# A two-layer diffusion backbone: the end of the first layer's expert mixture, with gates per expert and the overflow loop ahead of the last two experts

## The chip, the cores and the metric

The kernel runs on one core of one Trainium2 chip. The metric is device time in microseconds; the time before is the median of three runs. Engines are called as in the profile: PE (TensorE, matmuls), PEld (its weight loads), DVE (VectorE), ACT (ScalarE), POOL (GpSimd) and SP (SyncE, which here issues most DMA transfers).

## The reference, cut to what matters

Two layers, each a token mixer and then a mixture of experts, over 256 context and 256 latent tokens of width 1024. In the first layer both sets of tokens go through the mixture (512 tokens); each token goes to two of 32 experts. Context and latent tokens have gates of their own (`cgate2`, `gate2`).

```
def layer step (layer 0, second half):
    h = concat([layer_norm(xc) * (1 + cscale2) + cshift2, layer_norm(x) * (1 + scale2) + shift2])
    ffn = moe(h)          # sum over a token's two experts of w * (silu(h Wg) * (h Wu)) Wd
    xc = post_norm(ALPHA * xc + cgate2 * ffn[:256], ln2_g, ln2_b)
    x  = post_norm(ALPHA * x  + gate2  * ffn[256:], ln2_g, ln2_b)
```

Then layer 1 begins with `layer_norm` of both, a modulation, and the product with `w_in`.

## The kernel before

`moe(rt, keep)` is written once for both layers; `l` is the layer, and the change concerns `l == 0`, with `nt` = 4 tiles of 128 tokens. Tokens are gathered by expert in blocks of 64 rows. The loop runs over 34 experts: 0 to 19, then 32 and 33 (two spare blocks for experts with more than 64 tokens), then 20 to 31. An expert's weights are six loads of 1 MB (two halves each of gate, up and down), issued by SP in `load` (L1681) into a ring of 11 buffers. A load is issued when its buffer is free and when the transfer eight places earlier on SP has landed, since SP's transfers take turns on eight semaphores.

The work of one expert `e` in `expert0`: POOL gathers its tokens (L1688, `xg`), PE transposes them (`pxt`), ACT copies them out (`xgt`), PE forms gate and up in one PSUM tile (`pgu`, L1731), ACT and DVE make the SwiGLU (`th`, L1696 and L84), PE transposes it (`pat`, L1740), and PE multiplies by the down weights (`pd`, L1751). PE's order is interleaved: while expert `e` waits for its SwiGLU, gate of `e + 1` runs. ACT scales the result by the routing weight (`ye`, L93), and POOL scatters it to `yb_d` in DRAM (L1791), one row per token and choice.

Experts 30 and 31 don't go through DRAM. Their result stays as two rounded parts, `yh` (ACT) and `yl` (DVE), and PE multiplies both by a one-hot matrix `slt` into `po` (L1940), one 128x512 result for each tile and half; DVE adds these to `fa`, the sum of the token tile.

Behind that: `overflow` (L1514 on), a hardware loop over blocks that found no place in the spare ones. Its trip count is read from `ovi`, and with these inputs it is zero. Then the tail for each tile: gate (`g`), residual (`fx`, from `x1_d`, times `ALPHA`), statistics (L225, L226), affine step with `lg` and `lb`, and the store `x_d`. Layer 1's mixer normalises these tiles again (`bnnb`, `xh` on ACT, L242), transposes them on PE (`pht`, L482), and multiplies by `w_in` (`raw`, L516, split into `hi` on ACT and `lo` on DVE; `pfm`, L526 to L528).

Order around the change: a scheduler sets the order on each engine when the kernel is built. It doesn't move anything across a hardware loop. At the loop all engines meet, on the skip path too: SP goes on when the transfers that it issued have landed, and the others when everybody has arrived.

Of the kernel before, what the change touches and what calls it, by code (L numbers as in the profile page):

```python
# [11 lines left out]
F32 = mybir.dt.float32  # L12
# [9 lines left out]
D = 1024  # L22
# [30 lines left out]
def trunk(ctx: ExitStack, tc: tile.TileContext, A, out):  # L53
# [1285 lines left out]
    def route_start(l):  # L1339
        nt = 4 - 2 * l  # L1340

        def new(shape, name, dt=F32):
            return const.tile(shape, dt, tag="rt_" + name, name=name)

        rt = dict(l=l, nt=nt, both=new([128, 4, 32], "both")[:, :nt], ovi=new([1, 24], "ovi", I32))
        if l == 0:
            rt.update(oh=[new([128, 4, 32], f"oh{k}") for k in range(2)], wgt=new([128, 3, 4], "wgt"),
                      pos=new([128, 2, 4], "pos"), idx=new([128, 2, 32], "idx", I32), tok=new([128, 2], "tok"), wsl=new([128, 32], "wsl"),
                      sidx=new([128, 2, 2], "sidx", I32), swsl=new([128, 2], "swsl"),
                      pidx=pb("pidx")[:, :96])  # L1350
        else:

            rt.update(posx=new([128, 4, 32], "oh0")[:, :nt], wx=new([128, 4, 32], "oh1")[:, :nt])
        return rt
# [84 lines left out]
    def route_end(rt, wk):  # L1439
        if rt["l"] == 0:  # L1440
# [7 lines left out]
            V.tensor_copy(rt["wsl"], rt["pidx"][:, 64:96])  # L1448
            V.tensor_copy(rt["tok"], val[:, 0, 30:32])

    def route_over(rt, wk):
# [33 lines left out]
        for b in range(ns):  # L1485
# [23 lines left out]
            ts(val[:, 1:2], val[:, 1:2], 2.0, second, OP.mult, OP.add)  # L1509
            V.tensor_copy(rt["sidx"][:, :, b], val)  # L1510
            V.tensor_copy(rt["swsl"][:, b:b + 1], pi[:, 2:3])

    def overflow(rt, acc, g2):
# [4 lines left out]
        with ExitStack() as ph:  # L1518
            wk = ph.enter_context(tc.tile_pool(name=f"ov{l}", bufs=1))
            n = nc.values_load(ovi[0:1, NB:NB + 1], min_val=0, max_val=NB - ns)  # L1520
            with tc.For_i(0, n, 1) as b:  # L1521
# [75 lines left out]

                pg, pu = pa("pog"), pa("pou")
                for p, w in ((pg, A["moe_w_gate"]), (pu, A["moe_w_up"])):
# [11 lines left out]
                for nh in range(2):  # L1611
                    raw = load(A["moe_w_down"][l, ds(eb, 1), :, 512 * nh:512 * nh + 512])
                    p = pa("pod")
                    for k in range(4):
                        T.matmul(p[:rows], at_[:, k], raw[:, k], start=(k == 0), stop=(k == 3))
                    copyS(y[:rows, 512 * nh:512 * nh + 512], p[:rows], scale=wcol[:rows])
                slt = wk.tile([128, nt, 128], F32, name="oslt")
                if l == 0:
# [8 lines left out]
                for t in range(nt):  # L1627
                    for nh in range(2):
                        po = pc("opo")
                        cs = slice(512 * nh, 512 * nh + 512)  # L1630
                        T.matmul(po, slt[:rows, t], y[:rows, cs], start=True, stop=True)
                        if l == 1:
                            yg = wk.tile([128, 512], F32, tag="oyg", name="oyg")
                            tt(yg, po, g2[1][:, cs], OP.mult)
                            po = yg
                        tt(acc[t][:, cs], acc[t][:, cs], po, OP.add)

    def moe(rt, keep):
# [26 lines left out]
        if l == 0:  # L1665
            xg = [fx.tile([128, D], F32, name=f"xg{i}") for i in range(2)]
            for i in range(2):
                G.memset(xg[i], 0.0)
        else:
            acc = [fx.tile([128, D], F32, name=f"acc{t}") for t in range(nt)]  # L1670
# [100 lines left out]
        def expert0(e, xt, pgu, nxt):  # L1771
            y = wk.tile([128, 512], F32, tag="y", name="ye", bufs=3) if e not in (30, 31) else None
            front = nxt()
# [8 lines left out]
            down(p, e, a)  # L1782
            w = rt["wsl"][:, e:e + 1] if e < 32 else rt["swsl"][:, e - 32:e - 31]
            if e in (30, 31):
                yh, yl = y2[e - 30]
                copyS(yh, p, scale=w)
                stt(yl, p, w, yh, OP.mult, OP.subtract)
                return front
            copyS(y, p, scale=w)
            i = rt["idx"][:, 1, e:e + 1] if e < 32 else rt["sidx"][:, 1, e - 32:e - 31]  # L1790
# [110 lines left out]
        if l == 0:  # L1901

            pr3.close()
            bc = keep.enter_context(tc.tile_pool(name=f"fbc{l}", bufs=1, side="right", reuse_waits="tile"))
            pl2 = ExitStack()
            lp_ = pl2.enter_context(tc.tile_pool(name="last", bufs=1, side="right", reuse_waits="tile"))
            acc = [bc.tile([128, D], F32, name=f"fa{t}") for t in range(nt)]
            y2 = [[lp_.tile([128, 512], F32R, name=f"y{n}{i}") for n in "hl"] for i in range(2)]
# [8 lines left out]
        with tc.issue_after(rt["load"].ins):  # L1917
            if l == 0:
                xs = [bc.tile([128, D], F32, name=f"fx{t}") for t in range(2)]
                for t in range(2):  # L1920
                    y1 = lp_.tile([128, D], F32, tag="y1", name="y1", bufs=2)
                    for i, y in enumerate((acc[t], y1)):
                        dma(y, yb_d[ntok * i + 128 * t:ntok * i + 128 * t + 128, :])
                    tt(acc[t], acc[t], y1, OP.add)
                for t in range(2):
                    dma(xs[t], x1_d[128 * t:128 * t + 128, :])
                for t in range(2, nt):
                    dma(acc[t], yb_d[128 * t:128 * t + 128, :])
                g2 = {0: mod_bc(bc, l, 5, 0, "g20")}
            lg = bc_row(bc, part_bcast(A["ln2_g"][l], 128), "lg2")  # L1930
            lb = bc_row(bc, part_bcast(A["ln2_b"][l], 128), "lb2")
# [14 lines left out]
        pwk.close()  # L1946
        overflow(rt, acc, g2)
        fp = keep.enter_context(tc.tile_pool(name=f"fin{l}", bufs=2, side="right", reuse_waits="tile"))
        if l == 0:
            g2[1] = mod_bc(fp, l, 5, 1, "g21")  # L1950

        for t in range(nt):
            rows = slice(128 * t, 128 * t + 128)
            x = acc[t]
            if l == 0:
                f = tg if t else tt
                if t < 2:
# [98 lines left out]
```

## Time and profile before

| | us |
|---|---|
| runs: lowest, median, highest | 2517.08, 2523.96, 2527.08 |
| profiled execution, its own time | 2517.75 |
| its span | 2516.0 |
| PE busy | 2196.1 (87%) |
| DVE busy | 1414.9 (56%) |
| ACT busy | 693.1 (28%) |
| POOL busy | 544.6 (22%) |

The first mixture takes about 880 to 1434 us of the span, the seam behind it ends near 1487, where layer 1's first `pht` starts. The shares of the whole span mix stages with different limits, so the seam is read from rows of its own. The trace has two records for each of these matmul instructions: a half load of gate or up, eight instructions in the program, stands as x16.

### The profile page before, as it was taken

What the parts mean: (1) busy time and instruction counts of PE and PEld (TensorE: products, weight loads), DVE (VectorE), ACT (ScalarE), POOL (GpSimd) and SP (SyncE); (2) the same over time, 40 slices, a digit from 0 to 9 for tenths busy, and PEclk for the clock granted to TensorE, in tenths of its full rate; (3) what the DMA queues carried; (4) which work ended last, traced back from release to release, by engine and by line L of the source; (5) the groups of instructions that cost most, each with busy time, mean ns of one, the idle gap of its engine ahead of it and who ended that gap; (6) DMA issues with size and microseconds to landing.
All of it is one profiled execution on the core that took longest, in us unless ns stands there. A gap on an engine that the chain in (4) does not pass through costs nothing. (4 is left out here: it accounts for less than half of the span.)

```text
span 2516.0 us, 41430 instructions
## 1 busy us (share of the span) xinstructions
PE 2196.1 (87%) x16198; PEld 1525.2 (61%) x16198; DVE 1414.9 (56%) x2987; ACT 693.1 (28%) x1344; POOL 544.6 (22%) x486
## 2 busy tenths in 40 slices
PE   5899998999999699777688839997799779999996
PEld 3678766886657555444344437896777655555553
DVE  7958635657756720443432286456888755545445
ACT  2334412345552011111111113352365311111110
POOL 8989600022110301311011031001142100000000
PEclk8999999999999799889898969998899889999998
DMA  6643588657666699999999957649565699999996
GB/s 254 188 132 113 164 235 272 197 167 217 187 204 219 239 363 413 408 410 400 403 402 406 416 172 237 194 145 262 176 213 141 229 367 381 421 423 421 422 421 265
DMA packets 326999, 710.71 MB, mean 282 GB/s; under 512 B 40654, under 2 KB 240766, under 8 KB 274064
## 3 DMA queue, kind: packets, MB, share of 16 engines
q1 hardware_dynamic: 306576, 682.69, 75.4%
q10 hardware_dynamic: 14944, 17.27, 1.9%
q0 software_dynamic: 5280, 8.05, 1.0%
q8 instruction: 130, 2.13, 0.3%
q14 instruction: 69, 0.57, 0.1%
HBM read 645.82 MB, written 71.37 MB: 285 GB/s over the span
## 5 line engine op out<-in xcount | busy, mean ns | idle before, releaser
L1731 PE MATMUL pgu<-mraw,xgt 128*64 128x256 f32 x4224 | 507.3, 393 | 10.0 <-DMA mraw<-in_moe_w_up_dram 7.4
L1731 PEld LDWEIGHTS pgu<-mraw,xgt 128*64 128x64 f32 x4224 | 305.3, 141 | 193.1 <-issue 41.9
L526 PE MATMUL pfm<-hhi,hi 128*128 128x256 f32 (+1 forms) x832 | 284.0, 345 | 6.4 <-ACT hi L93 6.4
L528 PE MATMUL pfm<-hhi,lo 128*128 128x256 f32 (+1 forms) x832 | 281.8, 342 | 5.4 <-DVE lo L78 5.4
L527 PE MATMUL pfm<-hlo,hi 128*128 128x256 f32 (+1 forms) x832 | 284.1, 343 | 0.0
L78 DVE TENSOR_TENSOR lo<-raw,hi 128x1024 fp32r<-128x1024 f32 (+1 forms) x147 | 197.3, 1344 | 140.9 <-ACT hi L93 128.4
L1751 PE MATMUL pd<-mraw,at 128*64 128x512 f32 x1056 | 248.3, 604 | 17.4 <-ACT at L93 15.4
L93 ACT ACTIVATE hi<-raw 128x1024 fp32r<-128x1024 f32 (+1 forms) x160 | 169.3, 1059 | 222.0 <-PE pfm L527 119.6
L84 DVE SCALAR_TENSOR_TENSOR th<-th,pgu 128x256 f32<-128x256 f32 x132 | 55.5, 420 | 310.0 <-ACT th L1696 308.0
L526 PEld LDWEIGHTS pfm<-hhi,hi 128*128 128x128 f32 x832 | 158.6, 192 | 31.3 <-ACT hi L93 7.5
L528 PEld LDWEIGHTS pfm<-hhi,lo 128*128 128x128 f32 x832 | 158.4, 191 | 28.4 <-DVE lo L78 6.4
L527 PEld LDWEIGHTS pfm<-hlo,hi 128*128 128x128 f32 x832 | 158.9, 191 | 20.7 <-issue 4.7
L128 POOL TENSOR_TENSOR bnrs<-bnrs,mhalf 128x1 f32<-128x1 f32 x26 | 27.8, 1074 | 624.7 <-DVE bnrs L88 624.7
L1751 PEld LDWEIGHTS pd<-mraw,at 128*64 128x64 f32 x1056 | 72.4, 138 | 148.9 <-issue 108.2
L78 DVE TENSOR_TENSOR acc<-acc,po 128x512 f32<-128x512 f32 x124 | 79.6, 682 | 99.2 <-PE po L1839 99.1
L526 PE MATMUL pm<-yh,hi 128*128 128x512 f32 (+1 forms) x256 | 89.6, 363 | 8.8 <-DVE gatel L84 5.9
L527 PE MATMUL pm<-yl,hi 128*128 128x512 f32 (+1 forms) x256 | 90.8, 357 | 5.9 <-DVE yl L78 5.8
L526 PE MATMUL ptm<-hi,hhi 128*128 128x256 f32 x320 | 93.1, 291 | 0.0
L528 PE MATMUL ptm<-hi,hlo 128*128 128x256 f32 x320 | 92.7, 290 | 0.0
L84 DVE SCALAR_TENSOR_TENSOR yg<-pd,wcol,g 64x512 f32<-64x512 f32 x64 | 48.0, 750 | 78.8 <-PE pd L1751 78.4
L527 PE MATMUL ptm<-lo,hhi 128*128 128x256 f32 x320 | 92.2, 288 | 0.0
L528 PE MATMUL pm<-yh,lo 128*128 128x512 f32 (+1 forms) x256 | 88.8, 350 | 0.0
(533 smaller groups left out, 4131.0 us busy)
## 6 DMA issues: line engine op xcount, KB each, us to landing
mraw<-in_moe_w_gate_dram SPq DMA_DIRECT2D x132, 1024.0 KB
mraw<-in_moe_w_up_dram SPq DMA_DIRECT2D x132, 1024.0 KB
mraw<-in_moe_w_down_dram SPq DMA_DIRECT2D x132, 1024.0 KB
raw<-in_w_in_dram SPq DMA_DIRECT2D x116, 512.0 KB
modr<-in_mod_w_dram SPq DMA_DIRECT2D x80, 512.0 KB
modw<-in_mod_w_dram SPq DMA_DIRECT2D x8, 1024.0 KB
g_d<-gate SPq DMA_DIRECT2D x32, 256.0 KB
gtl<-gt_d SPq DMA_DIRECT2D x8, 1024.0 KB
```

The lines of the kernel that those rows point to most:

```text
L78: V.tensor_tensor(o, a, b, op=op)
L84: V.scalar_tensor_tensor(o, a, s, b, op0=op0, op1=op1)
L93: S.activation(o, a, AF.Copy, scale=scale)
L128: G.tensor_tensor(o, a, b, op=OP.pow)
L526: T.matmul(p, ahi, bhi, start=first, stop=False)
L527: T.matmul(p, ahi, blo, start=False, stop=False)
L528: T.matmul(p, alo, bhi, start=False, stop=last)
L1731: o = T.matmul(p[64 * cb:64 * cb + 64, 256 * i:256 * i + 256], xt[:, kt], raw[:, k, 256 * cb:256 * cb + 256], start=(kt == 0), stop=(kt == ...
L1751: o = T.matmul(p[64 * nh:64 * nh + 64], at[:, j, 64 * cb:64 * cb + 64], raws[cb][:, j, nh], start=(k == 0), stop=(k == 3))
```

## The change

1. `rt["cls"]` holds for each slot of each expert whether its token index is under 256 (context).
2. The gate is applied per expert: `g2n` holds both gate vectors in the layout of `pd`. For each expert DVE forms `gr` = gate vector by class (one tensor-scalar, one scalar-tensor-tensor and a 128x1 step) and `y` = `pd` times routing weight times `gr`. This takes the place of ACT's `ye` copy. For experts 30 and 31 `yh` is a copy of `y`, and `yl` the rest.
3. `fa` starts as `x1_d` times `ALPHA` (four loads by POOL's queue, four ACT steps), ahead of the loop.
4. `overflow` for layer 0 stands ahead of experts 30 and 31, and gates what it adds.
5. Behind expert 31, eight loads `ys` of `yb_d` by POOL's queue are added to `fa`: for tiles 0 to 2 by DVE, for tile 3 by POOL.
6. The tail's gates, residuals and `y` sums are gone, with their loads.

```
@@ route_end, route_over
+            ts(rt["cls"][:, :32], val[:, 0], 256.0, None, OP.is_lt)
+            ts(rt["cls"][:, 32 + b:33 + b], val[:, 0:1], 256.0, None, OP.is_lt)
@@ overflow
+                gg = g2
+                if l == 0:
+                    gg = [mod_bc(wk, l, 5, c, f"og{c}") for c in range(2)]
...
-                        if l == 1:
-                            yg = wk.tile([128, 512], F32, tag="oyg", name="oyg")
-                            tt(yg, po, g2[1][:, cs], OP.mult)
-                            po = yg
-                        tt(acc[t][:, cs], acc[t][:, cs], po, OP.add)
+                        yg = wk.tile([128, 512], F32, tag="oyg", name="oyg")
+                        tt(yg, po, gg[t // 2 if l == 0 else 1][:, cs], OP.mult)
+                        tt(acc[t][:, cs], acc[t][:, cs], yg, OP.add)
@@ moe
+            g2n = fx.tile([128, 2, 512], F32, name="g2n")
+            for c in range(2):
+                for nh in range(2):
+                    m = mods[0, 10 + nh, c, :]
+                    dma(g2n[64 * nh:64 * nh + 64, c], bass.AP(tensor=m.tensor, offset=m.offset, ap=[[0, 64], [1, 512]]))
@@ expert0
+            gr = wk.tile([128, 512], F32, tag="gr", name="gr", bufs=1)
+            c1 = wk.tile([128, 1], F32, tag="c1", name="c1")
+            ts(c1, rt["cls"][:, e:e + 1], -1.0, 1.0, OP.mult, OP.add)
+            ts(gr, g2n[:, 0], rt["cls"][:, e:e + 1])
+            stt(gr, g2n[:, 1], c1, gr, OP.mult, OP.add)
+            stt(y, p, w, gr, OP.mult, OP.mult)
             if e in (30, 31):
                 yh, yl = y2[e - 30]
-                copyS(yh, p, scale=w)
-                stt(yl, p, w, yh, OP.mult, OP.subtract)
+                copyS(yh, y)
+                tt(yl, y, yh, OP.subtract)
                 return front
-            copyS(y, p, scale=w)
@@ ahead of experts 30 and 31
+            acc = [bc.tile([128, D], F32, name=f"fa{t}") for t in range(nt)]
+            for t in range(nt):
+                G.dma_start(acc[t], x1_d[128 * t:128 * t + 128, :])
+                copyS(acc[t], acc[t], scale=ALPHA)
+            overflow(rt, acc, None)
@@ behind expert 31
-                xs = [bc.tile([128, D], F32, name=f"fx{t}") for t in range(2)]
-                for t in range(2):
-                    y1 = lp_.tile([128, D], F32, tag="y1", name="y1", bufs=2)
-                    for i, y in enumerate((acc[t], y1)):
-                        dma(y, yb_d[ntok * i + 128 * t:ntok * i + 128 * t + 128, :])
-                    tt(acc[t], acc[t], y1, OP.add)
...
+                for t in range(nt):
+                    for i in range(2):
+                        y = lp_.tile([128, D], F32, tag="ys", name="ys", bufs=6)
+                        G.dma_start(y, yb_d[ntok * i + 128 * t:ntok * i + 128 * t + 128, :])
+                        with tc.high_priority(offset=2000):
+                            (tg if t == 3 else tt)(acc[t], acc[t], y, OP.add)
...
-        overflow(rt, acc, g2)
+        if l:
+            overflow(rt, acc, g2)
...
-                f = tg if t else tt
-                if t < 2:
-                    f(x, x, g2[0], OP.mult)
-                    stt(x, xs[t], ALPHA, x, OP.mult, OP.add)
-                else:
-                    y = fp.tile([128, D], F32, tag="y", name="y")
-                    dma(y, yb_d[ntok + 128 * t:ntok + 128 * t + 128, :])
-                    f(x, x, y, OP.add)
-                    f(x, x, g2[1], OP.mult)
-                    xt = fp.tile([128, D], F32, tag="x", name="fx")
-                    dma(xt, x1_d[128 * t:128 * t + 128, :])
-                    stt(x, xt, ALPHA, x, OP.mult, OP.add)
             normed_affine(fp, x, x, lg, lb)
```

How the instructions stand now is shown at three places. A row is line, operation, result and operands, shape and count; `x8` of `pgu` is one half load. L1731, L1740, L1751 and L1940 of before are L1739, L1748, L1759 and L1954 of after.

PE before, from the transposes of expert 31's tokens on: first `pd` is expert 29's, the `x24` are both halves of `up` 30 and the first of gate 31, then `pd` of expert 30, its `po`, and `up` of 31. The loop stands some 30 rows further.

```order
L1760 MATMUL pxt<-identr,xg_8316 128x64 x8
L1731 MATMUL pgu<-mraw,xgt 64x256 x8
L1751 MATMUL pd<-mraw,at_11818 64x512 x8
L1731 MATMUL pgu<-mraw,xgt 64x256 x24
L1740 MATMUL pat<-identr,th 128x128 x2
L1731 MATMUL pgu<-mraw,xgt 64x256 x8
L1751 MATMUL pd<-mraw,at_11929 64x512 x8
L1940 MATMUL po<-yh_11851,slt 128x512
L1731 MATMUL pgu<-mraw,xgt 64x256 x8
L1940 MATMUL po<-yl_11852,slt 128x512
```

PE after, up to the loop: first the transpose of expert 29 and the last half of gate 30, `pd` of expert 29, and one half of `up` 30.

```order
L1748 MATMUL pat<-identr,th 128x128 x2
L1739 MATMUL pgu<-mraw,xgt 64x256 x8
L1759 MATMUL pd<-mraw,at_11982 64x512 x8
L1739 MATMUL pgu<-mraw,xgt 64x256 x8
L1522 TENSOR_LOAD ovi
L1523 COMPARE_AND_BRANCH
```

PE after, behind the loop: the transposes of expert 31's tokens, the other half of `up` 30 with the first of gate 31, then as before.

```order
L1768 MATMUL pxt<-identr,xg_8318 128x64 x8
L1739 MATMUL pgu<-mraw,xgt 64x256 x16
L1748 MATMUL pat<-identr,th 128x128 x2
L1739 MATMUL pgu<-mraw,xgt 64x256 x8
L1759 MATMUL pd<-mraw,at_12342 64x512 x8
L1739 MATMUL pgu<-mraw,xgt 64x256 x8
L1954 MATMUL po<-yh_12263,slt 128x512
L1954 MATMUL po<-yl_12264,slt 128x512
L1739 MATMUL pgu<-mraw,xgt 64x256 x8
```

So half of expert 30's work (half of `up`, and `down`) and all of expert 31's moved from ahead of the loop to behind it.

SP before, from expert 31's last four loads on (`up`, then `down`). The loop stands nine rows further.

```order
L1681 DMA mraw<-in_moe_w_up_dram 128x2048 x2
L1681 DMA mraw<-in_moe_w_down_dram 128x2048 x2
L1926 DMA fx_11992<-x1m_d 128x1024
L1926 DMA fx_11993<-x1m_d 128x1024
L213 DMA g_12006<-mods 128x2x512
L213 DMA lg_12008<-in_ln_g_dram 128x1024
L213 DMA lb_12010<-in_ln_b_dram 128x1024
L516 DMA raw<-in_w_in_dram 128x4x256 x3
L1923 DMA fa_11847<-yb_d 128x1024
```

SP after, from expert 31's gate on.

```order
L1689 DMA mraw<-in_moe_w_gate_dram 128x2048 x2
L1689 DMA mraw<-in_moe_w_down_dram 128x2048 x2
L1689 DMA mraw<-in_moe_w_up_dram 128x2048 x2
L1689 DMA mraw<-in_moe_w_down_dram 128x2048 x2
L213 DMA lg_12442<-in_ln_g_dram 128x1024
L213 DMA lb_12444<-in_ln_b_dram 128x1024
L1523 COMPARE_AND_BRANCH
L1523 UNCONDITIONAL_BRANCH x2
```

The weight loads keep their places, `fx` and `g` are gone, and the loop stands right behind `lb`; six `raw` follow behind the loop.

DVE before, from `yl` of expert 30 (`yl_11852`) to the loop; the four `fa` numbers are the four tiles.

```order
L84 SCALAR_TENSOR_TENSOR yl_11852<-pd,wsl,yh_11851 128x512
L84 SCALAR_TENSOR_TENSOR th<-th,pgu 128x256 x2
L84 SCALAR_TENSOR_TENSOR yl_11854<-pd,wsl,yh_11853 128x512
L78 TENSOR_TENSOR lo<-raw,hi 128x4x256 x3
L78 TENSOR_TENSOR fa_11847<-fa_11847,y_11994 128x1024
L78 TENSOR_TENSOR fa_11847<-fa_11847,po 128x512 x2
L78 TENSOR_TENSOR fa_11848<-fa_11848,y_11998 128x1024
L78 TENSOR_TENSOR fa_11848<-fa_11848,po 128x512 x2
L78 TENSOR_TENSOR fa_11849<-fa_11849,po 128x512 x2
L78 TENSOR_TENSOR fa_11850<-fa_11850,po 128x512 x2
L1520 TENSOR_LOAD ovi
```

DVE after, from `yl` of expert 31 (`yl_12266`) behind the loop to the first statistics; the four MEMSETs are short.

```order
L78 TENSOR_TENSOR lo<-raw,hi 128x4x256 x3
L78 TENSOR_TENSOR fa_12013<-fa_12013,ys 128x1024 x2
L78 TENSOR_TENSOR fa_12014<-fa_12014,ys 128x1024
L78 TENSOR_TENSOR fa_12013<-fa_12013,po 128x512 x2
L78 TENSOR_TENSOR fa_12014<-fa_12014,ys 128x1024
L78 TENSOR_TENSOR fa_12014<-fa_12014,po 128x512 x2
L78 TENSOR_TENSOR fa_12015<-fa_12015,ys 128x1024 x2
L78 TENSOR_TENSOR fa_12015<-fa_12015,po 128x512 x2
L78 TENSOR_TENSOR fa_12016<-fa_12016,po 128x512 x2
L225 BN_STATS bnst<-fa_12013 128x6
```

The sums, which stood ahead of the loop, stand behind it with six `ys` sums among them, and the statistics follow at once. POOL's order has the four `fa<-x1m_d` loads ahead of the scatters of experts 28 and 29, and these ahead of the loop; behind it come the eight `ys` loads and then the two sums of tile 3.

## Rows read from the trace of the kernel before

**Rows 1.** Windows in the mixture: stretch, length, busy us by engine, clock, DMA share, GB/s.
```profile
1180.00:1200.00 20.00, 16.52 (x128) 9.59 (x128) 1.78 (x4) 3.73 (x7) 2.93 (x3) 1.00 1.03 408
...
1380.00:1400.00 20.00, 20.00 (x152) 11.04 (x148) 0.84 (x2) 2.74 (x5) 2.02 (x2) 1.00 1.01 410
```

**Rows 2.** Waits in 900 to 1400: PE's, then SP's queue; total, times, longest.
```profile
PE pat L1740 <- DVE th L84: 40.7, 17, 8.7
...
SPq L1681 <- DMA mraw<-in_moe_w_gate_dram: 90.5, 28, 9.5
```

**Rows 3.** SP's issues at the seam: start, us, queue, line, operation, transfer, count.
```profile
1405.55 2.75 SPq L1681 DMA_DIRECT2D mraw<-in_moe_w_down_dram  x2
...
1418.33 0.33 SPq L213 DMA_DIRECT2D lg<-in_ln_g_dram  x1
1420.83 0.33 SPq L213 DMA_DIRECT2D lb<-in_ln_b_dram  x1
1423.50 7.94 SPq L516 DMA_DIRECT2D raw<-in_w_in_dram  x3
```

**Rows 4.** Timeline, experts 30 and 31: start, us, engine, instruction, idle before and releaser.
```profile
1413.91 0.51 PE L1740 MATMUL pat<-identr,th 128*128 128x128 f32 x2
...
1418.36 1.94 PE L1751 MATMUL pd<-mraw,at 128*64 128x512 f32 x8 [0.35 <-DMA mraw<-in_moe_w_down_dram]
...
1421.52 1.95 PE L1731 MATMUL pgu<-mraw,xgt 128*64 128x256 f32 x16
...
1433.48 0.75 DVE L84 SCALAR_TENSOR_TENSOR yl<-pd,wsl,yh 128x512 fp32r<-128x512 f32 x1 [6.38 <-ACT yh L93]
```

**Rows 5.** Windows at the seam: PE, PEld, DVE, ACT, POOL busy, clock, DMA.
```profile
1449.00:1455.00 6.00, 0.00 (x0) 0.00 (x0) 0.72 (x3) 0.00 (x0) 0.14 (x1) 0.50 0.47 167
1455.00:1486.00 31.00, 0.00 (x0) 0.00 (x0) 30.68 (x44) 0.32 (x1) 21.64 (x11) 0.50 0.26 101
```

**Rows 6.** Timeline of the tail behind `yl` of expert 31.
```profile
1437.38 3.88 DVE L78 TENSOR_TENSOR lo<-raw,hi 128x1024 fp32r<-128x1024 f32 x3 [3.14 <-DMA raw<-in_w_in_dram]
...
1457.16 3.31 POOL L81 TENSOR_TENSOR fa<-fa,y 128x1024 f32<-128x1024 f32 x1
...
1464.76 0.68 DVE L225 BATCH_NORM_STATS2 bnst<-fa 128x6 f32<-128x512 f32 x1
...
1486.97 0.90 PE L482 MATMUL pht<-identr,xh 128*128 128x128 f32 x3 [38.08 <-ACT xh L242]
```

**Rows 7.** Timeline around the two overflow loops, layer 0's and layer 1's.
```profile
1448.34 1.29 DVE L78 TENSOR_TENSOR fa<-fa,po 128x512 f32<-128x512 f32 x2 [0.37 <-PE po L1940]
1448.93 0.34 SPq L1962 DMA_DIRECT2D y<-yb_d  x1
...
1454.87 2.33 POOL L81 TENSOR_TENSOR fa<-fa,g 128x1024 f32<-128x1024 f32 x1 [44.06 <-DMA y<-yb_d]
1454.90 3.38 DVE L78 TENSOR_TENSOR fa<-fa,g 128x1024 f32<-128x1024 f32 x1 [5.28 <-DMA y<-yb_d]
...
2500.72 1.29 DVE L78 TENSOR_TENSOR acc<-acc,po 128x512 f32<-128x512 f32 x2 [0.71 <-PE po L1839]
2504.03 0.69 DVE L225 BATCH_NORM_STATS2 bnst<-acc 128x6 f32<-128x512 f32 x1 [2.03 <-issue]
```

**Rows 8.** PE's timeline where an expert starts behind an idle stretch.
```profile
1351.88 3.58 PE L1731 MATMUL pgu<-mraw,xgt 128*64 128x256 f32 x16
...
1358.87 1.22 PE L1760 MATMUL pxt<-identr,xg 64*128 64x64 f32 x8
```

**Rows 9.** Instructions of tiles `fa`, `slt`, `ye`: count, ns min/median/max, first and last start.
```profile
L78 DVE TENSOR_TENSOR fa<-fa,po x8: 680/682/690, 1442.9 to 1448.9; 128x512 f32<-128x512 f32 x8
...
L78 DVE TENSOR_TENSOR fa<-fa,y x2: 1226/1226/1226, 1441.6 to 1444.2; 128x1024 f32<-128x1024 f32 x2
...
L88 DVE TENSOR_SCALAR slt<-k_slots,off x8: 275/278/280, 1374.8 to 1376.2; 128x128 fp32r<-128x128 f32 x8
...
L93 ACT ACTIVATE ye<-pd,wsl x30: 681/687/690, 895.4 to 1408.8; 128x512 f32<-128x512 f32 x30
```

More of the change, by code (lines that the diff above doesn't have):

```diff
@@ L1348, in route_start @@
                       pos=new([128, 2, 4], "pos"), idx=new([128, 2, 32], "idx", I32), tok=new([128, 2], "tok"), wsl=new([128, 32], "wsl"),
-                      sidx=new([128, 2, 2], "sidx", I32), swsl=new([128, 2], "swsl"),
+                      sidx=new([128, 2, 2], "sidx", I32), swsl=new([128, 2], "swsl"), cls=new([128, 34], "cls"),
                       pidx=pb("pidx")[:, :96])
@@ L1518, in overflow @@
         with ExitStack() as ph:
-            wk = ph.enter_context(tc.tile_pool(name=f"ov{l}", bufs=1))
+            wk = ph.enter_context(tc.tile_pool(name=f"ov{l}", bufs=1, side="left" if l else "right"))
             n = nc.values_load(ovi[0:1, NB:NB + 1], min_val=0, max_val=NB - ns)
@@ L1596, in load @@
                     return raw
-                pg, pu = pa("pog"), pa("pou")
+                pg, pu = pa("pog"), (pa if l else pc)("pou")
                 for p, w in ((pg, A["moe_w_gate"]), (pu, A["moe_w_up"])):
@@ L1612, in overflow @@
                     raw = load(A["moe_w_down"][l, ds(eb, 1), :, 512 * nh:512 * nh + 512])
-                    p = pa("pod")
+                    p = (pa if l else pc)("pod")
                     for k in range(4):
@@ L1771, in expert0 @@
         def expert0(e, xt, pgu, nxt):
-            y = wk.tile([128, 512], F32, tag="y", name="ye", bufs=3) if e not in (30, 31) else None
+            y = wk.tile([128, 512], F32, tag="y", name="ye", bufs=3)
             front = nxt()
@@ L1904, in moe @@
             bc = keep.enter_context(tc.tile_pool(name=f"fbc{l}", bufs=1, side="right", reuse_waits="tile"))
+            acc = [bc.tile([128, D], F32, name=f"fa{t}") for t in range(nt)]
[3 more added lines that the diff above has]
+            overflow(rt, acc, None)
             pl2 = ExitStack()
             lp_ = pl2.enter_context(tc.tile_pool(name="last", bufs=1, side="right", reuse_waits="tile"))
-            acc = [bc.tile([128, D], F32, name=f"fa{t}") for t in range(nt)]
             y2 = [[lp_.tile([128, 512], F32R, name=f"y{n}{i}") for n in "hl"] for i in range(2)]
@@ L1918, in moe @@
             if l == 0:
-                xs = [bc.tile([128, D], F32, name=f"fx{t}") for t in range(2)]
-                for t in range(2):
-                    y1 = lp_.tile([128, D], F32, tag="y1", name="y1", bufs=2)
-                    for i, y in enumerate((acc[t], y1)):
-                        dma(y, yb_d[ntok * i + 128 * t:ntok * i + 128 * t + 128, :])
-                    tt(acc[t], acc[t], y1, OP.add)
[L1925 to L1929, printed above, removed]
+                for t in range(nt):
[4 more added lines that the diff above has]
+                            (tg if t == 3 else tt)(acc[t], acc[t], y, OP.add)
             lg = bc_row(bc, part_bcast(A["ln2_g"][l], 128), "lg2")
@@ L1946, in moe @@
         pwk.close()
-        overflow(rt, acc, g2)
+        if l:
+            overflow(rt, acc, g2)
         fp = keep.enter_context(tc.tile_pool(name=f"fin{l}", bufs=2, side="right", reuse_waits="tile"))
-        if l == 0:
-            g2[1] = mod_bc(fp, l, 5, 1, "g21")
         for t in range(nt):
@@ L1954, in moe @@
             x = acc[t]
-            if l == 0:
-                f = tg if t else tt
-                if t < 2:
-                    f(x, x, g2[0], OP.mult)
-                    stt(x, xs[t], ALPHA, x, OP.mult, OP.add)
-                else:
-                    y = fp.tile([128, D], F32, tag="y", name="y")
-                    dma(y, yb_d[ntok + 128 * t:ntok + 128 * t + 128, :])
-                    f(x, x, y, OP.add)
-                    f(x, x, g2[1], OP.mult)
-                    xt = fp.tile([128, D], F32, tag="x", name="fx")
-                    dma(xt, x1_d[128 * t:128 * t + 128, :])
-                    stt(x, xt, ALPHA, x, OP.mult, OP.add)
             normed_affine(fp, x, x, lg, lb)
```

## Prediction

> **What bounds the kernel now.** The change sits in the first mixture and in the seam behind it, so I read the views in this order: busy time by stretch inside the mixture, what PE and SP's queue wait for there, SP's issues at the seam, then the seam row by row.
>
> In the middle and at the end of the mixture the DMA engines are full: share 1.01 to 1.03 at 408 to 410 GB/s [rows 1]. PE still has a full stretch now and then, and it waits for `th` at `pat` for 40.7 us of 500; SP's queue waits above all for earlier weight loads to land [rows 2]. One expert is six loads of 1 MB, or 6 x 2.56 = 15.4 us at 410 GB/s. PE's work for one is two halves each of gate, up and down at 1.8 to 1.95 us, and transposes of 0.5 and 1.2: 12 to 13 us. So inside the mixture a microsecond more on DVE, ACT or PE is covered, and a megabyte more costs 2.56 us.
>
> At the seam the last two loads (`down` of expert 31) are issued at 1405.55 [rows 3]. Each transfer of SP waits for the one eight before it, so the issues of `lg`, `lb` and the first `raw` at 1418.33, 1420.83 and 1423.50 mark three landings 2.5 us apart: second half of `down` 30, first and second of `up` 31. Two more at that spacing put the last weight at about **1428.4**. The trace does not show this landing by itself; it is an estimate, good to about 0.5 us.
>
> In those last 18 us PE works behind the loads as they land: `pd` of 30 waits for its second half until 1418.36, `up` 31 starts at 1421.52, and `yl` of 31 ends at 1433.48 + 0.75 = 1434.23 [rows 4], only 5.8 us after the last landing. That is what the reader should see: **almost all compute of the last two experts is hidden under their own weight loads**. What follows is not hidden: PE does nothing from 1449 to 1486 while DVE is 99% busy in 1455 to 1486 [rows 5], until the first `pht` of layer 1 at 1486.97 [rows 6]. From `yl` to `pht` that is 52.7 us, and the change aims at these.
>
> **The change, part by part.**
>
> *The loop's place.* The loop body never runs here (no row of its lines exists), but its skip path is a meeting of all engines. DVE ends its last sum at 1448.34 + 1.29 = 1449.63 and starts again at 1454.90, released by the landing of a `y` that SP issued at 1448.93; at the second loop, with no load outstanding, DVE goes from 2500.72 + 1.29 = 2502.01 to 2504.03 [rows 7]. So the bare meeting costs 2.0 us, and SP passes only when what it issued has landed. Now the order puts all twelve loads of experts 30 and 31 ahead of the loop on SP, with `lg` and `lb` behind them, while PE stands at the loop after the first half of `up` 30; the second half, gate 31, `down` 30 and all else of 31 come behind. PE reaches its branch at about 1410, two halves ahead of the `pat` at 1413.91 [rows 4] (up to 5 later behind the `x1` loads below), and must now wait for the last weight. The cover described above is gone.
>
> End of the loop: last weight 1428.4; plus four `x1` tiles of 0.5 MB, which POOL issues in the full stretch (2 MB at 410 GB/s = 5.1; 0 if they find gaps); plus `lg` and `lb`, each written to 128 partitions of 4 KB, 0.5 MB (2 x 1.28 = 2.6); plus 2.0 for the meeting (up to 5.0, the other loop). I take the full prices of the first two, since rows 1 show no gap, and 2.0 since nothing new is outstanding then: 1428.4 + 5.1 + 2.6 + 2.0 = **1438.1**. Bounds: 1433 to 1441.
>
> *PE's work behind the loop.* PE comes out of 23 to 28 us of idleness; in such a stretch the granted clock is 0.50 [rows 5], that is 1.2 of 2.4 GHz, and a half that takes 1.95 us takes 3.58 [rows 4, 8]. Chain: `pxt` 1.2 [rows 8]; second half of `up` 30 at 3.6; first half of gate 31 at 2.6 (between 1.95 and 3.58, the clock rising in it: my choice); `pat` 0.5 [rows 4]; second half of gate 31 at 1.9; `down` 30 twice 1.9. That is 13.6 to the start of `up` 31. From there to the end of `yl` 31 before took 1434.23 - 1421.52 = 12.7 with all weights there or just there [rows 4]; the gate puts one more step in the chain, `ye` on DVE ahead of `yh`, 0.75 like `yl`, less the 0.06 that a plain subtract saves: +0.7. Sum 27.0 (24 with a full clock throughout, 29 with 1.2 GHz longer). `yl` 31 ends at 1438.1 + 27.0 = **1465.1**, against 1434.23.
>
> *Sums and tail.* DVE then does three `lo` splits, 3.9 [rows 6]; six sums of `ys` at 1.23 and eight of `po` at 0.68 [rows 9], 7.4 + 5.4 = 12.8. The eight `ys` loads are issued at the loop's end and have landed by then, except the seventh and eighth, which need a buffer that the first sum frees. Their two sums are Pool's, 3.3 each [rows 6]. They cost DVE either way: beside Pool's multiply DVE's own took 3.38 where a sum alone takes 1.23 [rows 7, 9], 2.1 more, or DVE waits for Pool's second sum: seventh load issued at about 1470, landed at most 6 us later (as the `y` of rows 7), two sums of 3.3, so up to 1483 where DVE would be at 1480.5. I take 2.1 once (0 to 4.3). The Trainium skill (page "SBUF — State Buffer", section "Who interferes with whom") says that a DVE instruction with both inputs in SBUF and a GpSimd one that reads SBUF exclude each other for a whole instruction. Read so, each of two meetings would cost a whole 3.3 us, and the sums would be 19.4 instead of 14.9; the 3.38 fits the rule, as Pool's multiply there was itself only 2.33 long.
>
> Gone are the gate multiplies, the residuals and the sums behind the old loop. From the first statistics to `pht` took 1486.97 - 1464.76 = 22.2 [rows 6]. In the new order two residual steps of 1.2 leave that stretch, and the fourth tile's statistics and affine step (2 x 0.6 + 1.2) come ahead of the first `bnnb`; I leave it at 22.2 (21 to 24). `pht` at 1465.1 + 3.9 + 14.9 + 22.2 = **1506.1**, which is 19.1 later. Put otherwise: 30.9 lost ahead of `yl` 31, and 52.7 - 41.0 = 11.7 won behind it.
>
> *Gates per expert.* DVE gets `ye` 0.75 (by `yl`), `gr` twice (a tensor-scalar of 128x512: 0.28 at 128x128 [rows 9], so between 0.3 and 0.7; and one scalar-tensor-tensor, 0.75) and a 128x1 step: about 2 us per expert, 34 times 68 us. ACT loses 0.69 per expert. At 15.4 us per expert under full DMA this costs nothing; what it costs without that cover is the third rival. `g2n` adds 0.5 MB early in the mixture: 1.3 us if DMA is full there too, 0 if not; taken 0. The order of the first loads and of a few steps of layer 1's mixer shifts too; I allow two loads, 2 x 2.56, as +-5 and take 0.
>
> Sum: +19.1 on the profiled run, 2517.75, gives 2536.9. That run is 6.2 under the median of those shown, 2523.96, so on the median: **2543**.
>
> **The rivals.**
>
> *The drain is cheaper.* `x1` finds gaps (-5.1), PE comes back at full clock (-2.4), Pool and DVE don't meet (-2.1): +9.5, 2533. For it: POOL's queue is its own, and DMA falls short of full in single stretches. Against: rows 1, and the clock after every idle stretch.
>
> *The loop doesn't wait for the weights* (other side). If the meeting needs only the engines' arrival, or loads may cross it, PE passes at about 1410 + 5 + 2 = 1417 and its 27 us run beside the landings to 1444; then `pht` at 1444 + 41.0 = 1485, 2 us earlier, and with the cheap prices above up to 12 earlier: 2512 to 2522, not slower. The point: whether PE's second half of `up` 30 starts ahead of the last weight's landing. Against: SP's release by the `y` in rows 7, and that waiting SP holds everybody.
>
> *DVE's gate isn't covered.* If `pat` waits for a `th` queued behind `gr`, each expert pays up to 1.2 us on PE: with PE at 12 + 1.2 against 15.4 this stays hidden, unless slots come free later and DMA loses its lead; then 32 x 1.2 = 38 more, 2581. Against: PE has about 3 us of slack per expert.
>
> **How the numbers follow.** Forecast 0.72, its own range 2533 to 2553 from the bounds of the terms, taken as independent; cheaper drain 0.12; loop without waiting 0.11; uncovered gate 0.05. About 0.5% (12.6 us) is what a measurement of this kernel can tell from no change, so slower means above 2536.6 and faster below 2511.3. Slower: 0.67 of the forecast's 0.72 and the 0.05, 0.72. Same: the forecast's rest 0.05, the cheap drain 0.12, half of the loop without waiting, 0.05: 0.22. Faster: the other half with the mixture's start gaining 5, 0.06. The range for 8 in 10 reaches from 2528 (drain partly cheaper) to 2559 (loop 5.0, two meetings, start +5).
>
> **What would show it.** In the profile after: PE idle from 1410 to 1415 on until 1438 and all engines released together there, behind the last of `down`, `lg` and `lb`; then `pgu` at half clock; `yl` of 31 about 27 us behind the loop; `pht` 41 us behind that. DMA should be nearly idle while PE works through 31. It is wrong if PE's `pgu` goes on ahead of the last landing, if the loop ends before 1432, or if the experts' period within the mixture moves by more than 0.3 us.

## The result and the profile after

The changed kernel takes 2563.85 us (median of 4 runs, 2559.9 to 2566.18) against 2524.61 on the same chip: ratio 1.0155, 95% interval 1.0138 to 1.0173. That is 39 us slower. The forecast was 19 us slower, 2543, with a range that ended at 2559. The direction is right, and the size forecast is half of what came.

The seam looks as forecast. Windows of the changed kernel (stretch, length, busy us of PE, PEld, DVE, ACT, POOL, granted clock, DMA share, GB/s) show PE, DVE, ACT and POOL all idle while the DMA engines are full; these answer [rows 5]:

```profile
1435.00:1440.00 5.00, 0.00 (x0) 0.00 (x0) 0.00 (x0) 0.00 (x0) 0.00 (x0) 0.50 1.01 417
1440.00:1445.00 5.00, 0.00 (x0) 0.00 (x0) 0.00 (x0) 0.00 (x0) 0.00 (x0) 0.50 1.02 424
1445.00:1450.00 5.00, 0.00 (x0) 0.00 (x0) 0.00 (x0) 0.00 (x0) 0.00 (x0) 0.50 1.01 418
1450.00:1455.00 5.00, 0.00 (x0) 0.00 (x0) 0.00 (x0) 0.00 (x0) 0.00 (x0) 0.50 0.55 221
...
1453.00:1454.00 1.00, 0.00 (x0) 0.00 (x0) 0.00 (x0) 0.00 (x0) 0.00 (x0) 0.50 0.28 115
1454.00:1455.00 1.00, 0.00 (x0) 0.00 (x0) 0.00 (x0) 0.00 (x0) 0.00 (x0) 0.50 0.03 12
...
1455.00:1460.00 5.00, 4.54 (x24) 2.99 (x26) 1.93 (x12) 0.60 (x1) 3.28 (x6) 0.50 0.55 199
...
1500.00:1510.00 10.00, 0.00 (x0) 0.00 (x0) 10.00 (x19) 0.00 (x0) 3.02 (x2) 0.50 0.00 0
```

The transfers run out between 1450 and 1455; the last packet of SP's queue ends at 1454.4, and 1.0 us later everybody goes on. SP's issues say what stood last in its queue; they answer [rows 3]:

```profile
1429.16 2.78 SPq L1689 DMA_DIRECT2D mraw<-in_moe_w_down_dram  x2
1434.09 0.33 SPq L213 DMA_DIRECT2D lg<-in_ln_g_dram  x1
1437.46 0.33 SPq L213 DMA_DIRECT2D lb<-in_ln_b_dram  x1
1469.88 16.67 SPq L516 DMA_DIRECT2D raw<-in_w_in_dram  x6
```

And the timeline of the seam, PE and DVE with what released them; it answers [rows 4, 6, 7]:

```profile
1426.63 1.94 PE L1759 MATMUL pd<-mraw,at 128*64 128x512 f32 x8 [0.66 <-DMA mraw<-in_moe_w_down_dram]
...
1429.12 1.95 PE L1739 MATMUL pgu<-mraw,xgt 128*64 128x256 f32 x16 [0.55 <-DMA mraw<-in_moe_w_up_dram]
...
1455.40 0.38 DVE L88 TENSOR_SCALAR off<-tok 128x2 f32<-128x2 f32 x4 [24.73 <-SPq L1523]
1455.46 1.22 PE L1768 MATMUL pxt<-identr,xg 64*128 64x64 f32 x8 [24.40 <-SPq L1523]
...
1456.62 5.75 PE L1739 MATMUL pgu<-mraw,xgt 128*64 128x256 f32 x32
...
1481.71 0.69 DVE L78 TENSOR_TENSOR yl<-ye,yh 128x512 fp32r<-128x512 f32 x1 [0.70 <-ACT yh L93]
...
1482.66 3.50 DVE L78 TENSOR_TENSOR lo<-raw,hi 128x1024 fp32r<-128x1024 f32 x3 [0.22 <-ACT hi L93]
1486.07 3.61 DVE L78 TENSOR_TENSOR fa<-fa,ys 128x1024 f32<-128x1024 f32 x3
...
1492.92 5.64 POOL L81 TENSOR_TENSOR fa<-fa,ys 128x1024 f32<-128x1024 f32 x2 [3.54 <-DMA ys<-yb_d]
1493.32 6.32 DVE L78 TENSOR_TENSOR fa<-fa,ys 128x1024 f32<-128x1024 f32 x2
...
1499.75 2.48 DVE L78 TENSOR_TENSOR fa<-fa,po 128x512 f32<-128x512 f32 x4
1502.14 0.69 DVE L225 BATCH_NORM_STATS2 bnst<-fa 128x6 f32<-128x512 f32 x1
...
1523.57 0.90 PE L482 MATMUL pht<-identr,xh 128*128 128x128 f32 x3 [28.04 <-ACT xh L242]
```

Here the reader sees the drain by name: PE and DVE sat 24.4 and 24.7 us, released by SP's queue at the loop's line (L1523), and `yl` of expert 31 ends at 1481.71 + 0.69 = 1482.40, 27.0 us behind the loop.

But the absolute times are off from the first line on. This is SP's first weight load of the first mixture, in the kernel before and then in the changed one:

```profile
782.57 0.82 SPq L1681 DMA_DIRECT2D mraw<-in_moe_w_gate_dram  x2
```

```profile
798.29 0.82 SPq L1689 DMA_DIRECT2D mraw<-in_moe_w_gate_dram  x2
```

Up to this load every engine has the same instructions in the same order in both kernels, and it still comes 15.7 us later. The 48.1 us between the two profiled spans (2564.1 and 2516.0) are 15.7 ahead of the mixture, 20.9 from there to the first `pht` (1523.57 against 1486.97, less the 15.7; the mixture's start adds nothing), and 11.5 behind it. Of the 48.1, 9.2 belong to the choice of the executions that were profiled (one 2.3 over its median, one 6.9 under). So the question was where some 18 us outside the seam come from.

### The profile page after: what moved, and what is told of

It is laid out like the page before. It is cut to its first block, busy times and chain, and to the rows that moved or that the text cites. A ratio compares the mean times of both kernels' runs of the same rounds, so it can differ in the third digit from the quotient of the medians.

```text
span 2564.1 us, 41536 instructions
## 1 busy us (share of the span) xinstructions
PE 2205.4 (86%) x16198; PEld 1533.7 (60%) x16198; DVE 1476.7 (58%) x3125; ACT 677.0 (26%) x1316; POOL 546.1 (21%) x495
## 5 line engine op out<-in xcount | busy, mean ns | idle before, releaser
L1739 PE MATMUL pgu<-mraw,xgt 128*64 128x256 f32 x4224 | 511.6, 395 | 15.8 <-DMA mraw<-in_moe_w_gate_dram 9.1
L1739 PEld LDWEIGHTS pgu<-mraw,xgt 128*64 128x64 f32 x4224 | 308.8, 142 | 201.5 <-issue 48.4
L1759 PE MATMUL pd<-mraw,at 128*64 128x512 f32 x1056 | 249.5, 602 | 4.6 <-DMA mraw<-in_moe_w_down_dram 3.2
L1759 PEld LDWEIGHTS pd<-mraw,at 128*64 128x64 f32 x1056 | 73.3, 138 | 135.3 <-issue 108.4
L84 DVE SCALAR_TENSOR_TENSOR ye<-pd,wsl,gr 128x512 f32<-128x512 f32 x32 | 24.0, 750 | 165.8 <-PE pd L1759 154.1
L1704 ACT ACTIVATE th<-pgu 128x256 f32<-128x256 f32 x66 | 25.4, 384 | 336.3 <-PE pgu L1739 287.7
```

The source lines that it names most:

```text
L84: V.scalar_tensor_tensor(o, a, s, b, op0=op0, op1=op1)
L1704: S.activation(th, pg, AF.Tanh, scale=0.5)
L1739: o = T.matmul(p[64 * cb:64 * cb + 64, 256 * i:256 * i + 256], xt[:, kt], raw[:, k, 256 * cb:256 * cb + 256], start=(kt == 0), stop=(kt == ...
L1759: o = T.matmul(p[64 * nh:64 * nh + 64], at[:, j, 64 * cb:64 * cb + 64], raws[cb][:, j, nh], start=(k == 0), stop=(k == 3))
```

## The experiments

**1 and 2. The same two kernels again.** Is it the execution?

> The changed kernel unchanged, beside the kernel before on one chip. The seam (last weight to the first pht of layer 1) accounts for about 21 us of the difference by the traces; in the two profiles another 16 us lie ahead of the mixture, in instructions that stand in the same order in both kernels, and 11 us behind the first pht. If these are a matter of which execution was profiled, the first moe weight load issues near 785 here and the ratio comes out near 1.008 (21 us). If they belong to the kernel, it issues near 798 again and the ratio stays near 1.0155 (39 us).

> The kernel before, unchanged, for a second profile and the noise of the comparison: ratio 1.000 within 0.002. First moe weight load at 782.6 as in the first profile if that stretch belongs to the kernel; some 5 to 10 us later if executions differ there.

Measured: changed kernel 2561.42, ratio 1.0162 (1.0141 to 1.0184); kernel before 1.0004 (0.9991 to 1.0017). The gap stays, so it belongs to the kernel. The lead-in of one profile is a poor witness, though: the first weight load comes at 789.0 in the second profile of before and at 793.0 in the second of the changed kernel, where the first ones had 782.6 and 798.3. Stages are therefore compared below from a stage's own start.

**3 and 4. The loop back behind expert 31, and no loop at all.**

```
-            overflow(rt, acc, None)          # ahead of experts 30 and 31
...
-        if l:
-            overflow(rt, acc, g2)
+        overflow(rt, acc, g2)                # experiment 3; 4 keeps the "if l"
```

> The change with one part undone: the overflow loop of layer 0 stands behind expert 31's sums again; gates per expert, scaled residual and the sums stay. If the drain in front of the loop is what costs (my theory): yl of expert 31 ends about 6 us behind the last weight's landing instead of 27 behind the loop, the first pht comes about 25 us earlier than in the changed kernel, near 1.000 of before or 1 to 4 us under it if nothing else in the change costs. Rival, the gates per expert and the x1 loads cost in the mixture: it stays at 10 us or more over before. Rival, the excess outside the seam belongs to the changed kernel's layout: about 15 us over before.

> The change without layer 0's overflow loop (its work is left out; its trip count is zero with these inputs). Prices the meeting by itself: with the loop gone nothing stands between the sums and the norms, so 2 to 5 us less than with the loop behind expert 31, and about 27 to 30 us less than the changed kernel.

Measured: 1.0117 (1.0099 to 1.0136) and 1.0102 (1.0082 to 1.0121). (In experiment 3 the loop's own tiles also go back to the left-hand side, where the kernel before has them; those lines are not printed here.) Putting the loop back wins 12 us instead of 25, and leaves 31 over before. Without any loop 26 remain; so the meeting costs 5 by the medians and 4 by the ratios, whose intervals overlap. The drain is real, but more than half of the loss stays when the loop is gone. Each of the kernels with the indicator tile spends 504 to 509 us from `pht` to the next mixture's loads where before spends 496.

**5 and 6. An unused tile in the kernel before.** The only thing that the change does ahead of the first weight load is to allocate `cls` among the constants: 34 numbers, 136 bytes per partition, for which the program sets 160 aside. A partition's memory is given out from two ends; what is allocated later from the end of the constants (the left-hand side) starts 160 bytes higher. This is the program's layout; the traces hold no addresses.

```
-                      sidx=new([128, 2, 2], "sidx", I32), swsl=new([128, 2], "swsl"),
+                      sidx=new([128, 2, 2], "sidx", I32), swsl=new([128, 2], "swsl"), pad=new([128, 34], "pad"),
```

> The kernel before with one unused tile of 136 bytes per partition where the change puts its class indicator; nothing reads or writes it, and every left-hand tile allocated after it starts 160 bytes higher, no longer on a multiple of 256 bytes. Address theory: the mixers' stretches take longer as in the changed kernel, +10 to +25 us over before. Rival (the gate work and the reordered steps of layer 1's mixer cost it): same as before within 4 us.

> The same with 64 bytes, so that the tiles keep multiples of 64 but not of 256. Address theory with a grain of 64 bytes: same as before within 4 us. With a grain of 256 or more: +10 to +25 us as with 160. Rival that addresses don't matter: same as before in both.

Measured: 1.0068 (1.0045 to 1.0090) with 160 bytes, 14 to 17 us; 1.0048 (1.0031 to 1.0065) with 64 bytes, 12 us. A tile that nobody reads or writes makes the kernel slower, and a shift by 64 bytes is enough for it.

**7. The changed kernel with the addresses of before.** The indicator moves into the mixture's own pool, which is allocated behind the weight ring; one cast and one comparison of 128x32 make it there.

```
-swsl=new([128, 2], "swsl"), cls=new([128, 34], "cls"),
+swsl=new([128, 2], "swsl"),
...
+            rt["cls"] = fx.tile([128, 128], F32, name="cls")
+            V.tensor_copy(rt["cls"][:, 64:96], rt["idx"][:, 0])
+            ts(rt["cls"][:, :32], rt["cls"][:, 64:96], 256.0, None, OP.is_lt)
```

> The changed kernel with the class indicator kept in the mixture's own tiles, so that all tiles of both mixers and the weight ring have the addresses of before; loop still ahead of the last two experts. Address theory: about 20 us over before, the drain alone (first pht 20 us later, nothing outside the seam). Rival: still 40 us over before.

Measured: 2543.02, ratio 1.0087 (1.0066 to 1.0108), 22 us over before. So the change as its code reads, with the loop ahead of the last two experts, costs 22 us, and the tile's place another 17 to 19 (1.0155 or 1.0162 less 1.0087; each ratio is good to about 5 us).

The page of the profile shows the effect. The row of SP's hardware queue gives packets, MB and the share of 16 engines' span that the packets took. Four kernels: before; before with the unused 160 bytes; the changed kernel; the changed kernel with the old addresses.

```profile
span 2516.0 us, 41430 instructions
...
q1 hardware_dynamic: 306576, 682.69, 75.4%
```

```profile
span 2540.9 us, 41430 instructions
...
q1 hardware_dynamic: 306576, 682.69, 76.0%
```

```profile
span 2564.1 us, 41536 instructions
...
q1 hardware_dynamic: 304624, 675.88, 74.5%
```

```profile
span 2541.4 us, 41537 instructions
...
q1 hardware_dynamic: 304624, 675.88, 74.1%
```

Share times span over MB is the time that a megabyte takes: 2.779 us before, 2.829 with the same packets shifted by 160, 2.826 in the changed kernel, 2.786 with the old addresses. The share alone hides it, since the span grows too. The trace's single packets show it as well. The weights of the second mixture come in 24448 packets of 8192 bytes; their median is 309 ns in each of the five profiles with the addresses of before (experiments 8 and 9 below among them) and 313 in each of the seven shifted ones.

**8. Old addresses, and the loop back as well.**

> As the last, with the loop behind expert 31 again. Address theory: 8 us over before to 5 us under it (the seam of this order cost 4 to 6 us more than before in its first profile, with the shift). Rival: 30 us over before as with the shift.

Measured: 1.0054 (1.0034 to 1.0073), 14 us over before, outside what I expected by 6. The order around the loop explains part. Three parts of its timeline: SP's last weight issue and POOL's `ys` loads, PE's last wait, and DVE's sums:

```profile
1423.22 2.72 SPq L1691 DMA_DIRECT2D mraw<-in_moe_w_down_dram  x2
...
1431.34 3.30 POOL L1942 DMA_DIRECT2D ys<-yb_d  x6 [6.61 <-DMA yb_d<-ye,idx]
...
1451.18 1.94 PE L1761 MATMUL pd<-mraw,at 128*64 128x512 f32 x8 [0.44 <-DMA mraw<-in_moe_w_down_dram]
...
1469.47 6.11 DVE L78 TENSOR_TENSOR fa<-fa,ys 128x1024 f32<-128x1024 f32 x2
...
1480.22 0.69 DVE L225 BATCH_NORM_STATS2 bnst<-fa 128x6 f32<-128x512 f32 x1 [2.06 <-issue]
```

The last weight's second half was issued at about 1425.9 and lands at 1451.2, since six `ys` loads (3 MB, an estimated 7.7 us at the 410 GB/s of [rows 1]) and the `x1` tiles (5.1) share the DMA engines with the weights. With the loop ahead, the `ys` loads had to wait behind it and delayed nothing. So undoing the move gives less than the drain's price.

**9. Both repaired: loop behind, old addresses, tail loads behind the weights.**

```
-                G.dma_start(acc[t], x1_d[...])        # ahead of expert 30
-                copyS(acc[t], acc[t], scale=ALPHA)
...
+                    dma(acc[t], x1_d[128 * t:128 * t + 128, :])
                     for i in range(2):
-                        G.dma_start(y, yb_d[...])
-                            (tg if t == 3 else tt)(acc[t], acc[t], y, OP.add)
+                        dma(y, yb_d[...])
+                            if i: tt(acc[t], acc[t], y, OP.add)
+                            else: stt(acc[t], acc[t], ALPHA, y, OP.mult, OP.add)
```

> The last kernel (loop behind expert 31, addresses of before) with the x1 and ys loads on SP behind the last weight loads instead of on POOL ahead of and among them, the residual scaled in the first sum, and all sums on DVE. If the last weight comes as early as before and the sums are paced by 8.5 MB of loads behind it (21 us at 410 GB/s), the first pht is about 12 us earlier than before: 2505 to 2515, ratio 0.993 to 0.998. Rival, what is won at the seam is lost in layer 1's mixer (6 us longer in the last two profiles): same as before within 4 us.

Measured: 2519.4 against 2523.35, ratio 0.9984 (0.9968 to 1.0001): the fastest of all, by an amount that can hardly be told from none. Its timeline from `yl` on:

```profile
1442.92 0.69 DVE L78 TENSOR_TENSOR yl<-ye,yh 128x512 fp32r<-128x512 f32 x1 [0.69 <-ACT yh L93]
1447.65 3.84 DVE L78 TENSOR_TENSOR lo<-raw,hi 128x1024 fp32r<-128x1024 f32 x3 [4.03 <-ACT hi L93]
1451.41 1.22 DVE L84 SCALAR_TENSOR_TENSOR fa<-fa,ys 128x1024 f32<-128x1024 f32 x1
...
1467.73 0.69 DVE L225 BATCH_NORM_STATS2 bnst<-fa 128x6 f32<-128x512 f32 x1 [2.06 <-issue]
...
1489.21 0.90 PE L482 MATMUL pht<-identr,xh 128*128 128x128 f32 x3 [27.41 <-ACT xh L242]
```

From the mixture's first scatter to `pht` it takes 584.1 us where before takes 589.5 and 590.2: 6 won, of the 12 that I expected. `lo` stands ahead of the sums and waits 4 us for ACT's `hi`, which waits for its `raw`, and the sums, 14 us of pure DVE work, don't begin before; they are paced by DVE, not by the loads. The meeting behind them costs 2.06.

**10. Grain of the address.**

> The kernel before with an unused tile of 128 bytes: left-hand tiles on multiples of 128 but not of 256 bytes. If what counts is a multiple of 256 or 512: as with 64 bytes, 9 to 16 us over before. If a multiple of 128 is enough: same as before within 4 us, and the HW queue's time per MB is 2.78 us again instead of 2.81 to 2.83.

Measured: 1.0044 (1.0029 to 1.0058), 10 to 11 us, and 2.811 us per MB. A shift by 128 slows the kernel too. The granted clock does not explain it: it was 0.927 to 0.931 in these runs and 0.926 to 0.932 in those of the kernel before beside them. A shift by 256 wasn't run, so that a multiple of 256 is what counts stays unshown; the runs show that 64, 128 and 160 bytes each cost.

All stages side by side, us, each from the instruction that ends the stage before: first weight load to first scatter, to the scatter of expert 29, to the end of `yl` 31, to the first statistics, to the first `pht`, to the first weight load on SP of gate in the second mixture, to the end.

| kernel | scatter | expert 29 | `yl` 31 | statistics | `pht` | mixture 2 | end | us/MB |
|---|---|---|---|---|---|---|---|---|
| before | 114.9 | 512.3 | 24.4 | 30.5 | 22.2 | 495.6 | 533.5 | 2.779 |
| before again | 116.4 | 513.4 | 24.3 | 30.4 | 22.2 | 495.8 | 535.5 | 2.784 |
| before, 64 bytes | 117.7 | 510.4 | 28.1 | 30.6 | 22.2 | 494.7 | 536.3 | 2.806 |
| before, 128 bytes | 117.1 | 512.3 | 28.8 | 28.8 | 22.2 | 498.2 | 535.4 | 2.811 |
| before, 160 bytes | 116.5 | 513.4 | 27.5 | 30.8 | 22.2 | 499.8 | 536.9 | 2.829 |
| changed | 114.8 | 516.5 | 52.8 | 19.7 | 21.4 | 503.8 | 536.8 | 2.826 |
| changed again | 116.0 | 516.0 | 53.0 | 20.1 | 21.4 | 506.0 | 536.0 | 2.812 |
| loop back (3) | 115.7 | 516.9 | 33.1 | 24.3 | 21.5 | 505.9 | 536.0 | 2.811 |
| no loop (4) | 115.6 | 515.8 | 31.9 | 23.0 | 21.4 | 509.3 | 535.5 | 2.812 |
| old addresses (7) | 115.3 | 512.2 | 51.5 | 20.0 | 21.4 | 503.6 | 532.2 | 2.786 |
| and loop back (8) | 114.9 | 511.6 | 31.7 | 24.9 | 21.5 | 501.8 | 534.2 | 2.786 |
| tail loads on SP (9) | 115.5 | 512.7 | 25.8 | 24.1 | 21.5 | 496.4 | 532.0 | 2.779 |

The shift's price is spread: 3 to 4 us where the last weights land (24.4 to between 27.5 and 28.8), 4 in the mixture of the changed kernel (512 with the old addresses; the shifts in the kernel before show nothing there), up to 4 in layer 1's mixer, some 2 from the second mixture on, and in the lead-in, where the first weight load comes at 793.1 on the mean of seven shifted profiles and 788.7 of five others, with a scatter as large as that. One thing stays open: with the old addresses the changed kernel still takes 6 to 8 us more from `pht` to the second mixture than before (501.8 and 503.6 against 496), and experiment 9 doesn't. Some 4 to 5 of it comes in one part, from the last `pE` to the last `pY` on PE: 42.7 and 41.4 us in experiments 7 and 8, 38.2 in experiment 9, 37.2 and 37.6 in before. The scheduler's order of layer 1's mixer differs between before and all three. But the instructions of DVE, ACT and POOL there stand in nearly the same order in experiments 7 and 9, which differ by 7 us, so the order on these engines alone does not explain it. What does was not tried.

## Why the prediction was off

*What bounds the kernel, and the loop as a drain: right.* PE stands at the loop after one half of `up` 30 and is released by SP. On the base of the mixture's first scatter (15.6 us later than before) the loop ends at 1455.4 - 15.6 = 1439.8; the forecast was 1438.1. With the old addresses it ends 3 earlier than forecast (1437.96, in a profile whose first scatter is 3.0 later than before's), so about 4.6 of the 7.7 for `x1`, `lg` and `lb` was paid there.

*PE's work behind the loop: right to 0.1.* 27.0 forecast, 27.0 measured, at clock 0.50 in 1455 to 1460 as [rows 5] let expect: 1.2 of 2.4 GHz behind 24 us without work. That the sum fits to 0.1 is luck: `up` 31 starts 12.5 behind the loop (1467.94 on PE) instead of 13.6, and from there to the end of `yl` 31 it takes 14.5 instead of 13.4.

*Sums: 14.9 forecast, 16.1 measured* (1486.07 to 1502.14). DVE's two sums beside POOL's took 6.32 where 2.45 would do, so the one meeting of 2.1 was in fact two, at 1.9 each. The instructions of tile `ys`, with count, shortest/median/longest in ns, first and last start:

```profile
L78 DVE TENSOR_TENSOR fa<-fa,ys x6: 1218/1221/3246, 1486.1 to 1496.4; 128x1024 f32<-128x1024 f32 x6
L81 POOL TENSOR_TENSOR fa<-fa,ys x2: 2367/2782/3198, 1492.9 to 1495.4; 128x1024 f32<-128x1024 f32 x2
```

POOL's first sum met nobody at its start and took 2.37; its second started while DVE's sum was under way and took 3.20. Each of DVE's two ends 1.08 behind the end of one of POOL's (1496.36 behind 1495.28, 1499.64 behind 1498.56), as DVE's 3.38 in [rows 7] ended 1.08 behind POOL's 2.33. So the 3.3 that the prediction read from [rows 6] as the price of a POOL sum holds a wait for DVE. The rule that I quoted from the Trainium skill (page "SBUF — State Buffer", section "Who interferes with whom") has the two exclude each other for a whole instruction. The trace agrees: DVE's sums waited for what was left of POOL's, 1.96 and 2.16 us, and the 19.4 that the prediction worked out by the rule was too high through the 3.3.

*Norms: 22.2 forecast, 21.4 measured. Gates per expert: nothing, as forecast*; the stage to the scatter of expert 29 is 511.6 to 512.7 with them and old addresses, 512.3 and 513.4 without.

*What failed is a term that the sum didn't have.* The part on gates priced their instructions, and the order "of a few steps of layer 1's mixer" at 0 +-5; it asked nothing of where the indicator's tile lies. I took the part of the program that stands in the same order to take the same time. It doesn't: 160 bytes at the bottom of the allocation moved every later left-hand tile, and the queue takes 0.9 to 1.7% longer per megabyte (2.806 to 2.829 in the seven shifted profiles, 2.779 and 2.784 in before). That is 17 to 19 us by experiment 7, 14 to 17 by experiment 5, and about half of the loss. The second lapse is smaller: the steps of layer 1's mixer, taken at 0 with 5 allowed, cost 6 to 8 (from experiments 7 and 8, with the cause open).

*The seam's 19.1 was partly luck.* From the mixture's first scatter to `pht` the changed kernel takes 610.4 us and before 589.5, which is 20.9 more. With the old addresses it takes 605.1, which is 15.3 more than the mean of before's two profiles. So the forecast of the seam by itself was 4 too high, and the missing term filled the gap.

*The rivals.* The cheaper drain was half right on `x1`, and wrong on the clock and on the meeting of DVE and POOL. The loop does wait. The uncovered gate didn't happen. None of them was the rival that was missing.

*My theory of the experiments* also lost a point: I expected 25 us from putting the loop back and got 12 and 8. Part of what is missing are the loads that had been held behind the loop and then ran beside the last weights: when experiment 9 put them behind the weights, `yl` 31 ended 25.8 instead of 31.7 us behind the scatter of expert 29. The rest has no account: with the old addresses the first `pht` came 15.4 earlier, seen from the mixture's first scatter (589.7 against 605.1), and the medians gained 8. The price of a wait isn't what its removal brings.

## What to carry to other kernels

In this kernel a hardware loop is a meeting even when its body never runs, and whatever SP has in flight is drained there: put such a loop where little is in flight and where no work is hidden under the loads, or behind such a place. When a change allocates a tile that lives from the start, look at where everything allocated after it then starts, and put the tile last, or in a pool of the stage that uses it; compare the time per megabyte of the DMA queue (share times span over MB) between two profiles before looking for a cause in the code. And if instructions in an unchanged order take longer, that is a finding of its own and not noise, once a second profile repeats it.

## What the runs showed of the hardware

- Where a tile starts within a partition matters for DMA. With left-hand tiles where the kernel before has them, the queue takes 2.779 to 2.786 us per MB (five profiles); 64, 128 or 160 bytes higher it takes 2.806 to 2.829 (seven profiles), and the kernel before is 10 to 17 us slower with shifts alone (1.0044 to 1.0068). By single packets: 8192 bytes of the second mixture's weights take 309 ns at the median in the five and 313 in the seven, with each of the three shifts; packets of 256 bytes take 18 to 24 in the five and 27 to 41 in the seven. Not every transfer is touched: the first mixture's weights have a median of 309 in all twelve, and so have, in the lead-in, packets of 1024, 2048 and 4096 bytes theirs (46, 84 and 159 ns).
- The mean packet here is 2227 bytes (682.69 MB in 306576). The Trainium skill (page "DMA: Bandwidth & Descriptors", section "How a descriptor splits into AXI transactions") says that a descriptor which doesn't start on a multiple of 256 bytes begins its first transaction at the boundary below and pays for the unused bytes, in beats of 32; it speaks of what a transaction reads. An estimate from that page: 2, 4 and 5 beats more on some 70, or 3, 6 and 7% for 64, 128 and 160 bytes. The runs agree in that shifts by 64 and 128 cost; they show 0.9, 1.1 and 1.7% over the mean of the two profiles of before, a fifth to a third of that estimate. That 160 costs more than 64 is not shown: the intervals of the times overlap, and two profiles of the changed kernel differ by 0.5% (2.826 and 2.812). The transactions themselves no run here shows.
- DVE and POOL adds of 128x1024 with all inputs in SBUF wait for each other: DVE's 1.22 us become 3.04 and 3.25, and DVE's ends 1.08 behind POOL's each time.
- The meeting at a loop with zero iterations costs 2.0 to 2.1 us between DVE's neighbours in the traces (2.03, 2.06, 2.06), and 4 to 5 us of the whole time (experiment 3 against 4, with intervals that overlap). With transfers in flight it lasts until the last of them has landed: 24.4 us without work on PE, with 1.0 us behind the queue's last packet.
- The lead-in of about 785 us, with instructions and addresses unchanged, differs between single profiles by up to 14.5 us (782.6 to 797.1 at the first weight load), so a stage is compared from its own start.
